# A planned hybrid RWKV-7 / gated DeltaNet block: new planner costs, modulation along the free axis, merged operations, seeded ranks

## The chip, the cores and the metric

The kernel runs on one core of a Trainium2 chip. The metric is the device time in microseconds of one execution; times are given as the median of several runs.

## The reference

One layer of a diffusion backbone over 256 latent tokens and 256 context tokens, with a model width of 2048. All inputs are fp32.

```python
mod = silu_c @ w_ada + b_ada                # 6 x 2048: shift, scale, gate, twice
mod_ctx = silu_cc @ w_ada + b_ada
sh1, sc1, gt1, sh2, sc2, gt2 = split(mod, 6)
h  = modulate(rmsnorm(x, norm1_w), sh1, sc1)
hc = modulate(rmsnorm(ctx, norm1_w), csh1, csc1)
y  = mix_tokens(h, hc, ...)                 # w_in, two mixers, gated merge, w_out
x  = x + gt1 * y
x  = x + gt2 * swiglu(modulate(rmsnorm(x, norm2_w), sh2, sc2), w_gate_up, w_down)
return rmsnorm(x, final_norm_w)
```

`mix_tokens` projects h and hc by `w_in`, runs a bidirectional RWKV-7 scan (16 heads of 64) and a bidirectional chunked gated DeltaNet (8 heads of 128, chunks of 64 here solved in blocks of 128 tokens), where the context's final states start the latent scans, projects both branches, merges them with sigmoid gates and applies `w_out`.

## The kernel before

**Products.** A large product is 128x128 weight tiles against 256 columns of tokens. Each fp32 weight tile is loaded as `wraw`, cast by ScalarE to a rounded high part `whi`, and VectorE subtracts to get the low part `wlo`. Three matmuls (high by high, high by low, low by high) make one fp32-like product. PSUM banks are named `mm` (3), `pa` (2), `pi` (1) and `s` (2).

**Stages by time.** From 0 to about 125 us the norms, the first two parts of the modulation (`ada_first`) and the low-rank columns of `w_in` are computed. From there to about 1340 us one planner, the class `Weave`, writes the instruction order of four engines: RWKV features, inverses and scans for 8 pairs of heads, then DeltaNet features, inverses and scans for 8 heads, with the products of `w_in` and of the merge between them. Then come `w_out` (to about 1440 us) and the FFN, in an order written by hand.

**The planner.** Each piece of work is a generator that yields operations, banks or names of events. `Weave.run` takes, again and again, the operation with the earliest start by its own model, and among equal starts the one with the lower rank. `Lane.cost` models durations, `Loads` (called as `dq`) issues a DMA on SP's queue and returns when the planner expects it to land, `Weave.through` models the fetching of PE's program in pieces. The order is fixed when the kernel is built; on the chip each engine runs its own queue in that order and waits on semaphores. A DMA is issued on SP's queue in the order of the plan too.

Pieces that the change touches:

- `lowrank` and `lowrank_out`: the low-rank products for 8 pairs, their sigmoid on ScalarE into four buffers `lo`, and the write of each to DRAM (`sgd_`), issued on ScalarE's queue.
- `invert`: triangular inverses by 16, 32, 64 blocks; with `full` (DeltaNet) both halves of the last step are made.
- `scan(r)`: four steps, in each of which pair r-1's latent part and pair r's context part run side by side (q is 0 and 1), from state buffers `VX`.
- `tokens`, `head_scan`: the same for DeltaNet, with two directions d.
- `features`: SiLU of a head's q, k, v, then a preload of the table for exp and ln.
- `ada_early`, `ada_rest`, and a last part in the loop over `w_out`: the modulation's columns 4096 to 10240 (gate 1, shift 2, scale 2). A tile has 128 input rows on the partitions and 512 or 1024 output columns; VectorE adds `tile * c[k]` to an accumulator over 16 tiles, and `ada_sum` then sums over the partitions:

```python
yield [e.matmul(ps[32 * j:32 * j + 32, 0:T], ones[:, 0:32], acc[:, T * j:T * j + T], ...) for j in range(nj)]
yield v.tensor_copy(arow[r], ps[r, 0:T])
yield [e.transpose(ps[:, T + P * q:...], arow[r, P * q:P * q + P], ident[r, r]) for q in range(2)]
for q in range(2):
    yield v.tensor_add(mod[:, o], ps[...:32], p_("bada")[:, o])
```

`ada_early` uses two weight buffers that the low-rank part has left (`spare`), and gives them to the ring of weight quarters (`raws`) when it ends.

Of the kernel before, what the change touches and what calls it, by code (L numbers as in the profile page):

```python
# [30 lines left out]
LAT = dict(dma=3.1, v=1.0, s=1.0, hop=dict(e=0.215, v=0.135, s=0.15, g=0.1), slack=0.1, own=0.09, grp=32, crank=-1, cg=4, into=0.14, back=0.2, cross=0.14, stay=0.0, gpace=1.6, fetch=3.7, least=0.2)  # L31
LNEXP = "natural_log_exp_and_others"
SIGM = "sigmoid_and_others"
WAITS = ((0, 1500, 7500, 12000, 13200), (16, 25, 147, 195, 199))
PIECE, EDGE, LEAD = 256, 193, 40
UNIT = 64 * 64 + 64
# [71 lines left out]
class Op:  # L108


    def __init__(self, lane, cost, call, mode=None, base=None, rows=0):
        self.lane, self.cost, self.call, self.mode, self.base, self.rows, self.left = lane, cost, call, mode, base, rows, None


class Lane:


    def __init__(self, engine, fixed, each, own, hop):
        self.engine, self.fixed, self.each, self.own, self.hop, self.base = engine, fixed, each, own, hop + LAT["slack"], None

# [31 lines left out]
    def __getattr__(self, name):  # L152

        def op(out, *a, **k):
            if name == "preload_act_table_set":
                return Op(self, 1.2, lambda: self.engine.preload_act_table_set(out))
            if name == "dma_start":
                return Op(self, 0.6 if self.each > 0.002 else 0.06, lambda: self.engine.dma_start(out, *a))
            mode, base, rows = None, None, rows_of(name, a[0]) if name in ("matmul", "transpose") else 0
# [6 lines left out]
            return Op(self, cost, lambda: getattr(self.engine, name)(out, *a, **k), mode, base, rows)  # L166
        return op
# [27 lines left out]
class Loads:  # L195


    def __init__(self, queue):
        self.queue, self.free = queue, 0.0

    def __call__(self, out, src, slow=1.0):
        self.queue.dma_start(out, src)
# [42 lines left out]
class Weave:  # L245


    def __init__(self):
        self.work, self.free, self.done, self.now, self.mode, self.cur, self.idle = [], {}, {}, 0.0, "full", None, True
        self.counted, self.asked, self.landed = None, -9.0, -9.0  # L250

    def add(self, rank, gen, at=None):
        now, cur = self.now, self.cur
        w = Piece(rank, gen, now if at is None else at)
# [84 lines left out]
    def run(self):  # L339
        while self.work:  # L340
# [40 lines left out]
            for o in ops:  # L381
# [19 lines left out]
def emit(ctx: ExitStack, tc, A, out, dbg=None):  # L401
# [141 lines left out]

    scr = [dpool.tile([2 * 8 * 2 * UNIT], F32, name=f"scr{i}") for i in range(2)]
# [3 lines left out]
    with tc.tile_pool(name="p0", bufs=1) as p0, \  # L548
# [7 lines left out]
        modc = p0.tile([P, 32], F32, name="modc")  # L556
        xt = p0.tile([P, KT, T], F32, name="xt")
# [23 lines left out]
        load_low(0)  # L581

# [125 lines left out]
    def invert(pool, Lt, parts, nu, which, full, fill, half_way=None, early=None):  # L708
# [84 lines left out]
        def out(t, d, h, ps, low):  # L793
# [9 lines left out]
        yield v.tensor_copy(qo, ps[:, 0:32 * h2].rearrange("p (i c) -> p i c", c=32))  # L803
        yield [e.matmul(ps[src, 32 * i:32 * i + 32], qo[dst, i, :], Tx[dst, u, cd], start=True, stop=True)
               for i, h, u, src, dst, cs, cd in quads]
        for h in range(2):
            yield [out(Tx, d, h, ps, True) for d in range(2)]
        weave.release(pib)
        if full:
            ps = yield pib  # L810
            yield [e.matmul(ps[dst, 32 * i:32 * i + 32], Tx[dst, u, cd], qo[dst, i, :], start=True, stop=True)
                   for i, h, u, src, dst, cs, cd in quads]
            for h in range(2):
                yield [out(T0, d, h, ps, False) for d in range(2)]
            weave.release(pib)
# [31 lines left out]
    half = (slice(0, 64), slice(64, 128))  # L847
    pr = [{} for _ in range(NPAIR)]
# [43 lines left out]
    def lowrank():  # L892
# [17 lines left out]
        out = [rs.tile([P, 8, 2, 64], F32, tag=f"VX{i}", name="lo").rearrange("p a b c -> p (a b c)") for i in range(2)]  # L910
        out = [t[:, n:n + 512] for t in out for n in (0, 512)]
# [19 lines left out]
    def prepare(p):  # L931
# [27 lines left out]
        for d in range(2):  # L959
# [19 lines left out]
            if not d:  # L979
# [4 lines left out]
                o["et"] = et = rs.tile([P, 16], F32, tag="et", name="et", bufs=3)  # L984
# [103 lines left out]
    VX = []  # L1088

    def scan(r):  # L1090
# [11 lines left out]
        if not VX:  # L1102
            VX.extend(rs.tile([P, 8, 2, 64], F32, tag=f"VX{i}", name="VX") for i in range(2))
# [12 lines left out]
        for m in range(4):  # L1116
# [6 lines left out]
            for q, o, n, vx, la, cs_ in todo:  # L1123
                for d, j, h in dh:
# [4 lines left out]
            R1 = rs.tile([P, T], F32, tag="y2", name="R1")  # L1129
# [11 lines left out]

            ops = []
# [4 lines left out]
            for q, o, n, vx, la, cs_ in todo:  # L1147
                if n >= 4:
                    for d, j, h in dh:
                        ops.append(add(acc[h, T + 64 * d:T + 64 * d + 64], j, vx[:, 4 * d + cm[d], j, :], la[d][:, cm[d], j, 64:P]))  # L1150
            if ops:
                yield ops
            for q, o, n, vx, la, cs_ in todo:
                for j, h in enumerate(half):
                    yield s.copy(vx[h, both, j, :], c3(ps[h, T + P * q:T + P * q + P]))
# [13 lines left out]
            for q, o, n, vx, la, cs_ in todo:  # L1169
                if n < 7:  # L1170
                    end = o["et"][:, cs_[0]:9 + cs_[1]:8 + cs_[1] - cs_[0]].unsqueeze(2)
                    i = (n + 1) % 4
                    for j, h in enumerate(half):
                        yield v.tensor_mul(VX[0 if n < 3 else 1][h, i:8 - i:7 - 2 * i, j, :], c3(acc[h, P * q:P * q + P]),
                                           end[h].to_broadcast([64, 2, 64]))
# [152 lines left out]
    def products():  # L1328
# [53 lines left out]
        while todo or ahead:  # L1382
# [70 lines left out]
            else:  # L1453
# [9 lines left out]
                  TF0=("VX0", 1024, 1), TF1=("VX1", 1024, 1), St0=("Y", T, 1), St1=("y3", T, 1), arow=("y2", T, 1))  # L1463
    first = {"LAl0": [P, 4, 2, P], "LAl1": [P, 4, 2, P], "LAc0": [P, 4, 2, 64], "LAc1": [P, 4, 2, 64], "Pm": [P, 2, 4, 64],
             "VX0": [P, 8, 2, 64], "VX1": [P, 8, 2, 64], "KBm": [P, 2, 4, 2, 64], "KBc": [P, 2, 4, 2, 64], "ivx": [P, 16, 64], "Y": [P, 4, 64], "R1": [P, 2, 64],
# [49 lines left out]
    def begin():  # L1515
# [48 lines left out]
        yield "scan", NPAIR - 1  # L1564
        for i in range(2):
            tf = gs.tile([P, 8, P], F32, name=f"TF{i}")
            yield g.memset(tf, 0.0)
            TF.append(tf)
# [27 lines left out]
    def features(h):  # L1596
# [16 lines left out]
        yield s.activation(k, k, AF.Silu)  # L1613
        yield s.activation(vq, vq, AF.Silu)
        yield s.preload_act_table_set(LNEXP)
# [4 lines left out]
    def tokens(h):  # L1620
# [18 lines left out]
        for d in range(2):  # L1639
            col = 8 * d + h  # L1640
            yield v.tensor_mul(kta[:, d], p4, eta[:, :, col:col + 1].to_broadcast([P, 4, P]))
# [103 lines left out]
    def head_scan(h):  # L1745
# [13 lines left out]
        for n in range(4):  # L1759
# [15 lines left out]
            for d in range(2):  # L1775
                yield v.tensor_scalar_mul(Vn[:, d, :], ps[:, P * d:P * d + P], btok[:, bs[d], 8 * d + h:8 * d + h + 1])
            weave.release(psb)
            if n < 3:
# [3 lines left out]
                for d in range(2):  # L1782
                    if n:
                        yield v.scalar_tensor_tensor(Sn[:, d, :], St[:, d, :], egl[:, bs[d], 8 * d + h:8 * d + h + 1],
                                                     ps[:, P * d:P * d + P], ALU.mult, ALU.add)
                    else:
                        yield v.tensor_copy(Sn[:, d, :], ps[:, P * d:P * d + P])
                weave.release(psb)
            if n >= 2:
# [3 lines left out]
                for d in range(2):  # L1793
                    y = O[:, bs[d], :]
                    if n == 2:
                        yield s.copy(y, ps[:, P * d:P * d + P])
                    else:
                        yield v.tensor_add(y, ps[:, P * d:P * d + P], y)
# [20 lines left out]
    NEARLY, NLATE = 6, 8  # L1819

    def ada_sum(b, nj, acc, arow):

        m = 2 * nj
        ps = yield pab
        yield [e.matmul(ps[32 * j:32 * j + 32, 0:T], ones[:, 0:32], acc[:, T * j:T * j + T], start=True, stop=True)
               for j in range(nj)]
        weave.ready("block", b)
        r = slice(0, 32 * nj)
        yield v.tensor_copy(arow[r], ps[r, 0:T])
        yield [e.transpose(ps[:, T + P * q:T + P * q + 32 * nj], arow[r, P * q:P * q + P], ident[r, r]) for q in range(2)]  # L1830
        for q in range(2):
            o = slice(32 + b + q, 32 + b + m, 2)
            yield v.tensor_add(mod[:, o], ps[:, T + P * q:T + P * q + 32 * nj:32], p_("bada")[:, o])
        weave.release(pab)
# [334 lines left out]
```

## Time and profile before

| what | value |
|---|---|
| median of 3 runs | 2189.05 us (2185.07 to 2195.54) |
| the profiled execution | 2184.15 us |
| its span | 2182.4 us |
| mean granted TensorE clock | 0.990 |
| instructions | 59116 |
| moved by DMA | 431.14 MB, mean 198 GB/s |

The span runs from the first to the last instruction of the core. PE is TensorE's matmul stream, PEld its weight loads, DVE is VectorE, ACT ScalarE, SP the engine that issues most DMAs; a q behind a name is the engine's sequencer. Nearly all planned operations carry line L166 or L188, those of the helpers that record them, so they are told apart by their tiles. A row of a group gives count, busy time and mean in ns, then the idle time before it and who ended it. A row of a wait gives total, times and longest in us.

### The profile page before, as it was taken

How to read it: one execution, taken by the hardware profiler on the slowest of the kernel's cores; microseconds unless marked ns; L12 is line 12 of the kernel's file. 1: busy time of each engine (PE TensorE's matmuls, PEld its weight loads, DVE VectorE, ACT ScalarE, POOL GpSimd, SP SyncE). 2: the span in 40 equal slices, each digit the busy share in tenths (PEclk: the TensorE clock that was granted, in tenths of full speed). 3: DMA queues.
4: the chain of work that ended last, by engine and by line, in shares of the span. 5: the costliest groups of instructions: out<-in, count | busy, mean ns of one | idle time of the engine just before them, and what ended most of it. 6: DMA issues, size and time to landing. Idle time of an engine off the chain costs nothing.

```text
span 2182.4 us, 59116 instructions
## 1 busy us (share of the span) xinstructions
PE 2104.8 (96%) x24536; PEld 1972.5 (90%) x24536; DVE 1551.1 (71%) x3305; ACT 1118.2 (51%) x2210; POOL 19.2 (1%) x55
## 2 busy tenths in 40 slices
PE   7999999999999999999999998999999999999997
PEld 5897699888898898998989998999999999999997
DVE  4466589889889976899988777865666665555554
ACT  3246655555556556556565755544444444444443
POOL 0000000000000000000000000000000000000000
PEclk9999999999999999999999999999999999999999
DMA  9966756645555554666644746847777776666665
GB/s 376 415 178 195 224 139 184 189 143 154 167 164 149 168 163 141 193 185 178 181 140 116 219 150 197 289 145 223 239 243 236 235 241 212 193 191 194 196 194 164
DMA packets 276813, 431.14 MB, mean 198 GB/s; under 512 B 119872, under 2 KB 137664, under 8 KB 272192
## 3 DMA queue, kind: packets, MB, share of 16 engines
q1 hardware_dynamic: 262720, 402.19, 60.0%
q10 hardware_dynamic: 13824, 25.17, 3.6%
q8 instruction: 192, 3.15, 0.6%
q14 instruction: 77, 0.63, 0.1%
HBM read 401.50 MB, written 25.77 MB: 196 GB/s over the span
## 4 chain that ended last, share of the span: by engine, by line
PE 78%; DVE 8%; DMA 8%; ACT 3%; issue 2%; SPq 0%; ACTq 0%; DVEq 0%
PE mm L188 62%; PE s L188 7%; PE pa L188 5%; PE pi L188 3%; DVE arena L166 2%; DMA wraw<-w 2%; DVE wlo L166 2%; DMA wraw<-ada_rest 1%; DMA wraw<-wgu 1%; ACT whi L166 1%; DMA wraw<-w_low 1%; ACT arena L166 1%; DMA aw<-ada_first 1%; DMA tscr<-arena 1%; DMA sgd__1597<-lo 0%
## 5 line engine op out<-in xcount | busy, mean ns | idle before, releaser
L500 DVE TENSOR_TENSOR wlo<-wraw,whi 128x1024 fp32r<-128x1024 f32 (+1 forms) x264 | 314.9, 1193 | 295.2 <-ACT whi L499 295.1
L499 ACT CAST whi<-wraw 128x1024 fp32r<-128x1024 f32 (+1 forms) x264 | 270.5, 1025 | 389.8 <-PE mm L188 354.8
L188 PE MATMUL mm<-hxh,wlo 128*128 128x256 f32 x1408 | 408.2, 290 | 8.3 <-DVE wlo L166 7.1
L188 PE MATMUL mm<-hxh,whi 128*128 128x256 f32 x1408 | 406.1, 288 | 2.0 <-ACT whi L166 1.0
L188 PE MATMUL mm<-hxl,whi 128*128 128x256 f32 x1408 | 403.9, 287 | 1.4 <-issue 1.4
L188 PE MATMUL mm<-hfh,wlo 128*128 128x256 f32 x1344 | 372.3, 277 | 2.6 <-DVE wlo L500 2.6
L188 PE MATMUL mm<-hfh,whi 128*128 128x256 f32 x1344 | 371.4, 276 | 0.0
L188 PE MATMUL mm<-hfl,whi 128*128 128x256 f32 x1344 | 371.2, 276 | 0.0
L166 ACT CAST whi<-wraw 128x512 fp32r<-128x512 f32 (+1 forms) x399 | 242.9, 615 | 201.1 <-PE mm L188 87.2
L166 DVE TENSOR_TENSOR wlo<-wraw,whi 128x512 fp32r<-128x512 f32 (+1 forms) x399 | 270.3, 680 | 88.5 <-ACT whi L166 85.6
L188 PEld LDWEIGHTS mm<-hxh,wlo 128*128 128x128 f32 x1408 | 266.0, 189 | 19.6 <-DVE wlo L166 11.4
L188 PEld LDWEIGHTS mm<-hxh,whi 128*128 128x128 f32 x1408 | 266.4, 189 | 10.3 <-issue 4.3
L188 PEld LDWEIGHTS mm<-hxl,whi 128*128 128x128 f32 x1408 | 266.2, 189 | 8.1 <-issue 5.7
L188 PEld LDWEIGHTS mm<-hfh,wlo 128*128 128x128 f32 x1344 | 252.4, 188 | 4.2 <-DVE wlo L500 4.0
L188 PEld LDWEIGHTS mm<-hfh,whi 128*128 128x128 f32 x1344 | 252.5, 188 | 0.2 <-ACT whi L499 0.2
L188 PEld LDWEIGHTS mm<-hfl,whi 128*128 128x128 f32 x1344 | 252.5, 188 | 0.0
L188 PE MATMUL mm<-za,whi 128*128 128x256 f32 x1024 | 175.2, 276 | 0.0
L188 PEld LDWEIGHTS mm<-za,whi 128*128 128x128 f32 x1024 | 154.1, 188 | 0.1
L188 PE MATMUL mm<-hch,wlo 128*128 128x256 f32 x528 | 151.1, 286 | 0.0
L188 PE MATMUL mm<-hcl,whi 128*128 128x256 f32 x528 | 150.9, 286 | 0.0
L188 PE MATMUL mm<-hch,whi 128*128 128x256 f32 x528 | 149.9, 284 | 0.0
L188 PE MATMUL mm<-za,wlo 128*128 128x256 f32 x512 | 141.3, 276 | 0.0
(389 smaller groups left out, 4173.4 us busy)
## 6 DMA issues: line engine op xcount, KB each, us to landing
wraw<-w SPq DMA_DIRECT2D x344, 256.0 KB, 3.3
wraw<-wgu SPq DMA_DIRECT2D x168, 512.0 KB, 4.6
aw<-ada_first SPq DMA_DIRECT2D x32, 1024.0 KB, 11.0
wraw<-wdn SPq DMA_DIRECT2D x64, 448.0 KB, 3.7
wraw<-ada_rest SPq DMA_DIRECT2D x96, 256.0 KB, 3.3
aw<-ada_rest SPq DMA_DIRECT2D x48, 512.0 KB, 4.2
wraw<-wout SPq DMA_DIRECT2D x64, 256.0 KB, 5.8
aw<-ada_gt ACTq DMA_DIRECT2D x64, 256.0 KB, 5.1
```

The costliest lines, as they stand in the source:

```text
L166: return Op(self, cost, lambda: getattr(self.engine, name)(out, *a, **k), mode, base, rows)
L188: return f(out, a, *x, **k)
L499: S.copy(hi[:, c, :M], raw[:, c, :M])
L500: V.tensor_sub(lo[:, c, :M], raw[:, c, :M], hi[:, c, :M].bitcast(F32))
```

## The change

- **Planner costs.** `Loads` counts KB, adds a landing time that grows with the transfer and with the KB still on their way; each ScalarE operation carries its table, and a change of table costs 1.28 us. A preload costs nothing else.
- **Seed.** Each piece added before the run and ranked under 800 gets its rank shifted by a number between -2 and 2, drawn with seed 84.
- **Modulation along the free axis.** `ada_rest` is laid out with 128 output columns on the partitions and the 2048 input rows along the free axis. SiLU of c goes to DRAM (`crow`) and is loaded broadcast to all partitions; one VectorE operation multiplies a tile by it and sums the products. `ada_sum` is gone, at all three places.
- **Merged operations.** In `scan`, the two q's state copies and state products become one each; `VX0` and `VX1` become one tile, as do `TF0` and `TF1` and the three `et`. In `tokens` and `head_scan`, two directions go in one operation.
- **Joined lists.** The last step of the full inverse writes both halves in one list, the second into a `pa` bank; the SiLUs and the preload are one list; in `scan` the readout matmuls on old states come ahead of the copy of R1.
- **Low-rank writes** are issued on SP's queue.

```diff
+NUDGE = (84, 2.0)
...
-                return Op(self, 1.2, lambda: self.engine.preload_act_table_set(out))
+                return Op(self, 0.0, lambda: self.engine.preload_act_table_set(out), table=out)
...
     def __call__(self, out, src, slow=1.0):
         self.queue.dma_start(out, src)
-        cost = int(np.prod(out.shape)) * 4 / 360e3 * slow
-        self.free = max(self.free, weave.now) + cost
-        return self.free + LAT["dma"] - weave.now
+        kb = int(np.prod(out.shape)) / 256
+        self.out = [x for x in self.out if x[0] > weave.now]
+        self.free = max(self.free, weave.now) + kb / 400
+        at = max(self.free + 1.8, weave.now + LAT["land"] + 0.0031 * kb + 0.0013 * sum(x[1] for x in self.out))
+        self.out.append((at, kb))
+        return at - weave.now
...
+        if cur is None and rank < 800:
+            rank += NUDGE[1] * (2 * self.draw.random() - 1)
...
+                if o.table is not None and o.table != lane.table:
+                    cost += LAT["table"]
+                    lane.table = o.table
...
-        yield s.dma_start(sgd_[p, :, j], so)
-        yield 2.5
+        yield dq(sgd_[p, :, j], so)
...
-            for q, o, n, vx, la, cs_ in todo:
-                for j, h in enumerate(half):
-                    yield s.copy(vx[h, both, j, :], c3(ps[h, T + P * q:T + P * q + P]))
+            for j, h in enumerate(half):
+                yield s.copy(vxs[h, :, both, j, :], states(ps[h, T + part.start:T + part.stop]))
...
-            for d in range(2):
-                yield v.tensor_scalar_mul(Vn[:, d, :], ps[:, P * d:P * d + P], btok[:, bs[d], 8 * d + h:8 * d + h + 1])
+            b2 = pick(btok.rearrange("p b c -> p (b c)"), 16 * bs[0] + h, 16 * bs[1] + 8 + h)
+            yield v.tensor_mul(Vn, ps[:, 0:T].rearrange("p (d c) -> p d c", d=2), b2.unsqueeze(2).to_broadcast([P, 2, P]))
...
+    def ada_half(w, cB, acc):
+        return v.scalar_tensor_tensor(w, w, 1.0, cB, ALU.mult, ALU.mult, accum_out=acc)
...
+        cB, w = (t.rearrange("p k m -> p (k m)") for t in spare[:2])
+        for q, to in enumerate((mod[:, 32:80], gq)):
+            yield dq(cB, crow[512 * q:512 * q + 512].partition_broadcast(P))
+            for i in range(48):
+                yield dq(w, A["ada_rest"][i, :, 512 * q:512 * q + 512])
+                yield ada_half(w, cB, to[:, i:i + 1])
...
+        yield dq(cB, crow[1024:2048].partition_broadcast(P))
...
+            yield dq(w, A["ada_rest"][i, :, 1024:2048])
+            yield ada_half(w, cB, gr[:, i:i + 1])
...
+                Q.dma_start(w, A["ada_rest"][48 - NLATE + i, :, 1024:2048])
+                V.scalar_tensor_tensor(w, w, 1.0, cB, ALU.mult, ALU.mult, accum_out=gr[:, i:i + 1])
```

More of the change, by code (lines that the diff above doesn't have):

```diff
@@ L1 @@
+import random
 import itertools
@@ L108, with __init__ @@
 class Op:
-    def __init__(self, lane, cost, call, mode=None, base=None, rows=0):
-        self.lane, self.cost, self.call, self.mode, self.base, self.rows, self.left = lane, cost, call, mode, base, rows, None
+    def __init__(self, lane, cost, call, mode=None, base=None, rows=0, table=None):
+        self.lane, self.cost, self.call, self.mode, self.base, self.rows, self.left, self.table = lane, cost, call, mode, base, rows, None, table
 class Lane:
     def __init__(self, engine, fixed, each, own, hop):
-        self.engine, self.fixed, self.each, self.own, self.hop, self.base = engine, fixed, each, own, hop + LAT["slack"], None
+        self.engine, self.fixed, self.each, self.own, self.hop, self.base, self.table = engine, fixed, each, own, hop + LAT["slack"], None, None
     def product(self, out, a):
@@ L155, in op @@
             if name == "preload_act_table_set":
[L156 removed]
+                return Op(self, 0.0, lambda: self.engine.preload_act_table_set(out), table=out)
             if name == "dma_start":
                 return Op(self, 0.6 if self.each > 0.002 else 0.06, lambda: self.engine.dma_start(out, *a))
[L159 removed]
+            mode, base, table, rows = None, None, None, rows_of(name, a[0]) if name in ("matmul", "transpose") else 0
             if name == "transpose" and len(a) == 2:
@@ L165, in op @@
                 cost, base = self.cost(name, out, a, k), (out.offset // out.ap[0][0], out.shape[0])
-            return Op(self, cost, lambda: getattr(self.engine, name)(out, *a, **k), mode, base, rows)
+            if name == "activation":
+                table = TABLES.get(a[1])
+            return Op(self, cost, lambda: getattr(self.engine, name)(out, *a, **k), mode, base, rows, table)
         return op
@@ L542, in emit @@
     S.activation(ck, ck, AF.Silu)
+    crow = dpool.tile([D], F32, name="crow")
     scr = [dpool.tile([2 * 8 * 2 * UNIT], F32, name=f"scr{i}") for i in range(2)]
@@ L556, in emit @@
         modc = p0.tile([P, 32], F32, name="modc")
+        c16 = p0.tile([16, P], F32, name="c16")
+        Q.dma_start(c16, A["cvec"].rearrange("(k p) -> k p", p=P))
+        S.activation(c16, c16, AF.Silu)
         xt = p0.tile([P, KT, T], F32, name="xt")
@@ L803, in invert @@
         yield v.tensor_copy(qo, ps[:, 0:32 * h2].rearrange("p (i c) -> p i c", c=32))
+        pf = (yield pab) if full else None
         yield [e.matmul(ps[src, 32 * i:32 * i + 32], qo[dst, i, :], Tx[dst, u, cd], start=True, stop=True)
-               for i, h, u, src, dst, cs, cd in quads]
+               for i, h, u, src, dst, cs, cd in quads] + [
+            e.matmul(pf[dst, 32 * i:32 * i + 32], Tx[dst, u, cd], qo[dst, i, :], start=True, stop=True)
+            for i, h, u, src, dst, cs, cd in quads if full]
         for h in range(2):
-            yield [out(Tx, d, h, ps, True) for d in range(2)]
+            yield [out(Tx, d, h, ps, True) for d in range(2)] + [out(T0, d, h, pf, False) for d in range(2) if full]
         weave.release(pib)
         if full:
[L810 to L815, printed above, removed]
+            weave.release(pab)
         return N_, Nt_, Tx
@@ L847, in emit, with pick @@
     half = (slice(0, 64), slice(64, 128))
+    def pick(t, i, j):
+        end = j + 1 if j > i else j - 1
+        return t[:, i:None if end < 0 else end:j - i]
+    ets = rs.tile([P, 3, 16], F32, tag="et", name="et")
     pr = [{} for _ in range(NPAIR)]
@@ L909, in lowrank @@
             weave.release(b)
-        out = [rs.tile([P, 8, 2, 64], F32, tag=f"VX{i}", name="lo").rearrange("p a b c -> p (a b c)") for i in range(2)]
-        out = [t[:, n:n + 512] for t in out for n in (0, 512)]
+        out = rs.tile([P, 2, 8, 2, 64], F32, tag="VX", name="lo").rearrange("p i a b c -> p (i a b c)")
+        out = [out[:, n:n + 512] for n in range(0, 2048, 512)]
         for p in range(NPAIR):
@@ L1102, in scan @@
         if not VX:
-            VX.extend(rs.tile([P, 8, 2, 64], F32, tag=f"VX{i}", name="VX") for i in range(2))
+            VXS.append(rs.tile([P, 2, 8, 2, 64], F32, tag="VX", name="VX"))
+            VX.extend(VXS[0][:, i] for i in range(2))
         if more:
@@ L1128, in scan, with add @@
             yield ops
+            acc = yield psb
+            fresh = [True, True]
+            def add(o, j, x, y, stop=False):
+                start, fresh[j] = fresh[j], False
+                return e.matmul(o, x, y, start=start, stop=stop)
+            if last:
+                yield [add(acc[h, T + 64 * d:T + 64 * d + 64], j, vx[:, 4 * d + cm[d], j, :], la[d][:, cm[d], j, 64:P])
+                       for q, o, n, vx, la, cs_ in todo if n >= 4 for d, j, h in dh]
             R1 = rs.tile([P, T], F32, tag="y2", name="R1")
@@ L1168, in scan @@
             yield ops
[L1169 to L1175, printed above, removed]
+            going = [q for q, o, n, *_ in todo if n < 7]
+            if going:
+                i = (m + 1) % 4
+                ends = [(r - 1 + q) % 3 * 16 + m + 4 * q for q in going]
+                ends = [pick(ets.rearrange("p i c -> p (i c)"), x, x + 11 - 2 * m) for x in ends]
+                end = bass.AP(ends[0].tensor, ends[0].offset, [ends[0].ap[0], [ends[-1].offset - ends[0].offset or 1, len(going)], ends[0].ap[1], [0, 64]])
+                to = VXS[0][:, 1 if m == 3 or going[0] == 0 else 0].unsqueeze(1) if len(going) == 1 else VXS[0][:, ::-1]
+                for j, h in enumerate(half):
+                    yield v.tensor_mul(to[h, :, i:8 - i:7 - 2 * i, j, :], states(acc[h, P * going[0]:P * going[-1] + P]), end[h])
             if last:
@@ L1792, in head_scan @@
                        enumerate(((St[:, d, :], Qe[:, d, P * bs[d]:P * bs[d] + P]), (Vn[:, d, :], PT[:, d, bs[d], :])))]
[L1793 to L1798, printed above, removed]
+                y, both = (O if n == 2 else O[:, ::-1]), ps[:, 0:T].rearrange("p (d c) -> p d c", d=2)
+                yield s.copy(y, both) if n == 2 else v.tensor_add(y, both, y)
                 weave.release(psb)
@@ L1815, in head_scan @@
             Q.dma_start(dbg["ob"][:, h, :], ob[:, h, :])
[L1819 to L1834, printed above, removed]
+    NLATE = 8
+    gq = apad[:, 0:48]
+    def ada_half(w, cB, acc):
+        return v.scalar_tensor_tensor(w, w, 1.0, cB, ALU.mult, ALU.mult, accum_out=acc)
     def ada_early():
         yield ("spare",)
-        ws = [t.rearrange("p k m -> p (k m)") for t in spare[:2]]
-        for b in range(NEARLY):
-            for k in range(KT):
-                w, last = ws[k % 2], ws[1 - k % 2]
-                yield dq(w, A["ada_rest"][b // 2, :, k, 512 * (b % 2):512 * (b % 2) + 512])
-                if k:
-                    yield v.scalar_tensor_tensor(w, w, ck[:, k, 0:1], last, ALU.mult, ALU.add)
-                else:
-                    yield s.activation(w, w, AF.Identity, scale=ck[:, 0, 0:1])
-            yield from ada_sum(4 * b, 2, w, last[:, 0:T])
+        cB, w = (t.rearrange("p k m -> p (k m)") for t in spare[:2])
[4 more added lines that the diff above has]
+                yield ada_half(w, cB, to[:, i:i + 1])
         raws.put(*spare[:2])
+        yield v.tensor_add(gq, gq, p_("bada")[:, 32:80])
+        yield v.tensor_add(mod[:, 32:80], mod[:, 32:80], gq)
+        weave.ready("halves")
         yield "turned", NPAIR - 1
@@ L1855, in ada_rest @@
         yield "out", NPAIR - 1
-        acc, kx = [gs.tile([P, 1024], F32, tag="KBc", name="aw") for _ in range(2)]
+        cB, kx = [gs.tile([P, 1024], F32, tag="KBc", name="aw") for _ in range(2)]
         ws = [gs.tile([P, 1024], F32, tag="KBm", name="aw") for _ in range(2)]
@@ L1967, in emit @@
         at = (KT - NB) * NGH // CG
-        acc = mp.tile([P, 1024], F32, name="acc")
-        adds = dict(zip((1, 2, 4, 6, 8, 10, 12, 13), range(KT - NLATE, KT)))
+        cB = mp.tile([P, 1024], F32, name="cB")
+        gr = mp.tile([P, NLATE], F32, name="gr")
+        Q.dma_start(cB, crow[1024:2048].partition_broadcast(P))
+        adds = dict(zip((1, 2, 4, 6, 8, 10, 12, 13), range(NLATE)))
         for j in range(KT):
```

96 lines of the change are left out of this document (32 added, 64 removed).

## The prediction, made before the change was run

> **What bounds the kernel now.** I read the page's busy shares and chain first, then the busy time by stage, then what the tensor engine waited for, then the costliest groups.
>
> ```profile
> span 2182.4 us, 59116 instructions
> PE 2104.8 (96%) x24536; PEld 1972.5 (90%) x24536; DVE 1551.1 (71%) x3305; ACT 1118.2 (51%) x2210; POOL 19.2 (1%) x55
> PE 78%; DVE 8%; DMA 8%; ACT 3%; issue 2%; SPq 0%; ACTq 0%; DVEq 0%
> ```
>
> TensorE is the bound, and 96% busy leaves 77.6 us idle. A busy PE isn't a dense PE, so the idle time is a lower bound for what a better order can recover. Busy time by stage (window, length, PE, PEld, DVE, ACT, POOL, clock, DMA share, GB/s) shows where it lies:
>
> ```profile
> 125.00:260.00 135.00, 126.05 (x909) 100.33 (x910) 80.21 (x175) 83.17 (x155) 2.41 (x7) 0.97 0.65 199
> 260.00:500.00 240.00, 233.21 (x3615) 212.95 (x3614) 211.48 (x497) 130.06 (x332) 6.02 (x18) 1.00 0.58 163
> 500.00:750.00 250.00, 244.43 (x4240) 221.53 (x4239) 226.80 (x533) 136.44 (x358) 8.48 (x23) 1.00 0.57 160
> 750.00:950.00 200.00, 197.72 (x2571) 179.42 (x2568) 156.88 (x385) 123.80 (x283) 1.90 (x2) 0.99 0.58 170
> 950.00:1150.00 200.00, 189.60 (x2350) 176.22 (x2350) 180.98 (x488) 117.47 (x263) 0.00 (x0) 0.97 0.57 163
> 1150.00:1340.00 190.00, 183.87 (x2181) 175.52 (x2179) 146.73 (x398) 108.80 (x239) 0.00 (x0) 0.98 0.56 172
> 1340.00:1440.00 100.00, 95.94 (x819) 92.82 (x817) 80.76 (x138) 60.15 (x108) 0.00 (x0) 1.00 0.80 263
> 1440.00:2182.00 742.00, 726.23 (x6342) 723.29 (x6342) 413.39 (x550) 321.61 (x407) 0.00 (x0) 0.99 0.67 205
> ```
>
> Length less PE busy: 9.0, 6.8, 5.6, 2.3, 10.4, 6.1 in the planned (woven) stretch to 1340, 4.1 in the out projection, 15.8 in the FFN, which the change doesn't touch. So 40 us of PE idle lie where the plan decides. VectorE is 88%, 91% and 90% busy in the windows at 260, 500 and 950: nearly a second bound there. What PE waits for is scattered; the largest waits of 125 to 1440, and ScalarE's largest wait for a transfer (over the span):
>
> ```profile
> PEld s L188 <- ACT lo L166: 12.6, 18, 2.0
> PEld mm L188 <- DVE wlo L166: 11.4, 20, 1.7
> PE mm L188 <- DVE wlo L166: 7.1, 15, 1.5
> ACT whi L166 <- DMA wraw<-w: 73.9, 51, 3.2
> ```
>
> The casts are placed earlier than their quarters land, 51 times, and VectorE's low halves and PE's matmuls queue behind.
>
> **The modulation sums.** Before, a sum over 128 input rows is made by ones-matmuls, a copy, two transposes and two adds, nine times in the woven stretch and once in the out projection. PE's timeline at the first:
>
> ```profile
> 378.17 0.63 PE L188 MATMUL pa<-wraw,CR 128*32 128x256 f32 x4
> 378.73 0.39 PE L188 MATMUL mm<-hxh,wlo 128*128 128x256 f32 x1
> 378.95 0.28 PE L188 MATMUL mm<-hxh,whi 128*128 128x256 f32 x1
> 379.07 0.28 PE L188 MATMUL mm<-hxl,whi 128*128 128x256 f32 x1
> 381.25 0.33 PE L188 MATMUL pa<-C,wraw 64*128 64x64 f32 x2
> 381.51 0.38 PE L188 MATMUL mm<-hxh,whi 128*128 128x256 f32 x1
> ```
>
> The matmuls hold PE from 378.17 to 378.73 (0.56), the next matmul takes 0.22 where 0.12 is usual (0.10 for the return), the transposes 0.26: 0.92 us. Ten of them are 9 us, all on the bound engine: **-9**. A bank of the pair "pa" comes free each time.
>
> What replaces them is the same number of loads and one VectorE operation with an accumulated sum per tile.
>
> ```profile
> L166 DVE SCALAR_TENSOR_TENSOR wraw<-wraw,ck 128x512 f32<-128x512 f32 x90 | 66.8, 743 | 16.2 <-DMA wraw<-ada_rest 15.7
> L166 DVE SCALAR_TENSOR_TENSOR aw<-aw,ck 128x1024 f32<-128x1024 f32 x37 | 47.0, 1270 | 0.0
> L2051 DVE SCALAR_TENSOR_TENSOR aw<-aw,arena 128x512 f32<-128x512 f32 x64 | 41.5, 686 | 0.0
> L2051 DVE DVE_READ_ACCUMULATOR aw<-aw,arena 128x1 f32 x64 | 5.3, 82 | 0.0
> L166 ACT ACTIVATE wraw<-wraw,ck 128x512 f32<-128x512 f32 x6 | 4.3, 724 | 0.1
> L202 SPq DMA_DIRECT2D wraw<-ada_rest x96: 327/328/3016, 248.6 to 933.9; - x96
> ```
>
> L2051 is the same operation already in use for gt2: 686 + 82 ns. Early tiles: 96 x 0.768 = 73.7 against 66.8, so +7 on VectorE. Later ones have no row at 1024 with an accumulator; between 2 x 0.686 and the 1.27 of the scaled form, plus 0.08, I take the nearer form, 1.30 (bounds 1.3 and 1.45): 40 x 1.30 = 52 against 47.0, +5 (at most +11). ScalarE loses nine first tiles, 4.3 us for six. The nine sums' copies (0.42 each, by the rows of that width below) and narrow adds (0.1 each, an estimate) leave VectorE: 9 x 0.62, -5.5. The early loop stays serial, each load behind the last operation, as now: 685 us for 96 loads. The plan's landing grows from 3.8 to 4.1 or more, 96 x 0.3 = 29 us later if that paced it, and six sums leave its chain, each 3.3 us or more by the timeline above; so the two buffers it holds return at about the same time, and I book zero.
>
> [...]
>
> Three broadcast loads of c and its round trip through DRAM are added. In the opening one more SP issue (0.4 us) stands ahead of x; in the out projection 512 KB more pass where the DMA share is 0.80 (2 us at its 263 GB/s). Together between 0 and 3, I take **+1.5**.
>
> **Merged operations.** Rows of the pieces, and rows of the widths that they become:
>
> ```profile
> L166 ACT COPY VX<-s 64x128 f32<-64x128 f32 x128 | 33.2, 260 | 33.8 <-PE s L188 31.5
> L166 ACT COPY VX<-pa 64x256 f32<-64x256 f32 x64 | 23.5, 367 | 8.9 <-PE pa L188 8.1
> L166 DVE TENSOR_TENSOR VX<-s,et 64x128 f32<-64x128 f32 x112 | 32.2, 287 | 9.6 <-PE s L188 7.2
> L166 DVE TENSOR_TENSOR LAc<-pa,C 64x256 f32<-64x256 f32 x32 | 13.5, 421 | 0.7
> L166 DVE TENSOR_SCALAR Vn<-s,btok 128x128 f32<-128x128 f32 x64 | 21.6, 344 | 8.2 <-PE s L188 8.0
> L166 DVE TENSOR_TENSOR arena<-pa,C 128x256 f32<-128x256 f32 x32 | 13.3, 415 | 0.6 <-PE pa L188 0.4
> ```
>
> State copies: 128 become 56 wide and 16 narrow, 56 x 0.367 + 16 x 0.260 = 24.7, -8.5 on ScalarE. State products: 112 become 42 and 28, 42 x 0.421 + 28 x 0.287 = 25.7, -6.5 on VectorE. Vn: 32 x 0.415 = 13.3, -8.3. Outputs, first states and kta also go in pairs, 3.5 on VectorE as an estimate by the same steps (some 0.15 us for each of 24 operations less). VectorE's sum is 7 + 5 - 5.5 - 6.5 - 8.3 - 3.5 = -12. Between no effect (cover by products) and all of it, I take 60%, since half the stretch runs at 90% VectorE: **-7**. The readout matmuls moved ahead of the copy and the shared list of the inverse keep their count; they trade one wait for a bank held longer, bounds -5 to +5, I take 0.
>
> **Low rank writes move from ScalarE's queue to SP's.** ScalarE's timeline in that stage:
>
> ```profile
> 173.44 0.69 ACT L166 ACTIVATE lo<-s,PR 128x512 f32<-128x512 f32 x1 [1.03 <-DMA sgd__1597<-lo]
> 174.16 0.33 ACTq L158 DMA_DIRECT2D sgd__1597<-lo  x1
> 174.59 0.69 ACT L166 ACTIVATE lo<-s,PR 128x512 f32<-128x512 f32 x1 [0.46 <-ACT lo L166]
> 175.29 1.28 ACT L156 ACT_TABLE_LOAD   x1
> 175.31 0.33 ACTq L158 DMA_DIRECT2D sgd__1597<-lo  x1
> 176.59 0.51 ACT L166 ACTIVATE sgd<-raw,om 64x256 f32<-64x256 f32 x1
> ```
>
> Each issue keeps ScalarE from its next operation for 0.46 us: 32 x 0.46 = 15 us in the window 125 to 260. PE's 12.6 us of waiting for "lo" stand against it; a third goes, **-4** (bounds 0 and -12). SP now waits for each activation, with weight loads queued behind it: the slower rival.
>
> **The plan.** The planner now lets a 256 KB quarter land after 4.1 us plus 0.33 for each other one on its way, instead of 3.8; it charges each change of ScalarE's table; the seed shifts ranks by up to 2. None of it is work. Bounds: 0, or a loss like the gain where the new order fits worse, and 40 - 7 - 4 = 29 us, all idle that the other terms leave. I take somewhat over a third of it, since the 51 late casts are what the landing term addresses and most of PE's waits are for other things: **-11**. "Program pieces" stand in the planner already; that part of the title changes nothing.
>
> ```profile
> L166 ACT ACT_TABLE_LOAD x14 | 18.0, 1283 | 1.4 <-DMA arena<-gts__1615 1.2
> ```
>
> These 14 loads, which came with an activation, had no cost in the plan: 18 us of ScalarE that arrived unplanned. In the rows above the load ends at 176.57 and the next activation starts at 176.59, so 1.28 is the whole price, as the plan now has it. [...]
>
> **The sum.** -9 + 1.5 - 7 - 4 - 11 = -29.5 against the profiled execution's 2184.15: 2154.6. The median of the runs is 4.9 above that execution: **2159 us**. About 0.5% (11 us, the runs' own scatter) can't be told from no change.
>
> **Rivals.** (1) The order absorbs the savings: VectorE and ScalarE relief stays under products and the plan's idle only moves. Then PE's 9 us less 1.5 remain: 2189 - 7.5 = 2181. For it: idle is spread over many small waits with no single cause. Against it: VectorE at 90%.
> (2) The plan is better than booked: with true landings the casts run ahead, VectorE's relief counts in full, and PE returns less often from small to full matmuls at 0.1 us each. All 40 us of idle and 9 of sums: 2189 - 49 + 1.5 = 2141, and 15 us less, 2126, if 150 returns fall away. For it: 73.9 us of ScalarE waiting for quarters. Against: only 18 us of PE's waits name "wlo".
> (3) Slower: SP stands at each of the 32 writes until its activation is done, as PE waits for it now up to 2.0 us, and the quarter behind it lands late. 32 x 2.0 = 64 us of SP, which the raw quarters on hand cover in part; if half reaches PE and the plan and ScalarE's relief give nothing, 2189 + 32 - 14.5 = 2206. It decides from 0.45 us of each write on PE (14.5 us, what the sums and VectorE give). Against it: the plan places the write where it expects the activation to end.
>
> **How the numbers follow.** Forecast 0.50 (2142 to 2176), rival 2 0.18, rival 1 0.22 (2178 to 2200), rival 3 0.10. Faster by over 0.5%: 0.50 + 0.18 + a little of rival 1, 0.70; same 0.20; slower 0.10. The range goes from 2128, in rival 2, to 2194, in rival 1, and leaves out rival 3 and the lower half of rival 2, under 2 in 10.
>
> **What would show it.** PE instructions fall by some 80 and no matmul reads ones for the sums; the state copies count 72 and ScalarE's waits for "wraw<-w" fall well under 73.9; PE idle from 125 to 1340 falls from 40 to 25; the FFN stays as it is. The prediction is wrong if SP's own waits grow from 165 to 255 with PE idle there over 9.0, if accumulating tiles take over 0.8 us, or if PE idle before 1340 stays at 40 with VectorE less busy.

## The result, and the profile after

The changed kernel takes 2170.67 us (median of 6 runs, 2165.26 to 2176.36) against 2188.86 for the kernel before beside it: ratio 0.993, interval 0.9906 to 0.9954. That is 18 us of the 29.5 forecast. The head of its page, with the shares of the chain:

```profile
span 2170.1 us, 58874 instructions
PE 2085.1 (96%) x24460; PEld 1963.9 (90%) x24460; DVE 1535.1 (71%) x3335; ACT 1103.2 (51%) x2140; POOL 21.5 (1%) x55
PE 73%; DMA 11%; DVE 9%; ACT 4%; issue 3%; SPq 1%; DVEq 0%; ACTq 0%
```

The span is 12.3 us shorter, PE busy 19.7 less, so PE's idle time grew from 77.6 to 85.0 us. By stage:

```profile
125.00:260.00 135.00, 123.34 (x906) 98.95 (x906) 79.27 (x173) 79.58 (x149) 2.42 (x7) 0.99 0.62 191
260.00:500.00 240.00, 230.02 (x3693) 210.80 (x3691) 209.46 (x511) 126.52 (x311) 7.23 (x20) 0.99 0.58 162
500.00:750.00 250.00, 241.17 (x4169) 219.54 (x4170) 223.51 (x550) 132.71 (x336) 9.58 (x21) 0.99 0.55 156
750.00:950.00 200.00, 196.76 (x2501) 181.43 (x2500) 155.10 (x410) 121.16 (x275) 1.85 (x2) 0.98 0.56 168
950.00:1150.00 200.00, 194.05 (x2471) 184.35 (x2471) 179.38 (x478) 115.28 (x250) 0.00 (x0) 1.00 0.61 184
1150.00:1340.00 190.00, 180.57 (x2106) 171.12 (x2105) 148.00 (x392) 115.51 (x249) 0.00 (x0) 0.97 0.58 179
1340.00:1440.00 100.00, 95.66 (x806) 93.76 (x806) 82.55 (x150) 59.10 (x109) 0.00 (x0) 0.98 0.82 269
```

Length less PE busy is 11.7, 10.0, 8.8, 3.2, 6.0, 9.4 in the planned windows: 49.1 us where 40 stood and 25 were forecast. Only the window at 950 gained. The first FFN matmuls, in the timelines of before and of after, show that the whole gain lies ahead of the FFN:

```profile
1443.26 0.50 PE L188 MATMUL mm<-hfh,w 128*128 128x256 f32 x2 [2.07 <-ACT hfh L2018]
```

```profile
1431.57 0.51 PE L193 MATMUL mm<-hfh,w 128*128 128x256 f32 x2 [2.07 <-ACT hfh L2009]
```

They start 11.7 us earlier; from there to the end it is 739.1 and 738.5 us. The waits of after that answer to those quoted before (the first over the span, the others from 125 to 1440):

```profile
ACT whi L171 <- DMA wraw<-w: 93.7, 57, 6.2
PEld mm L193 <- DVE wlo L171: 18.9, 27, 1.7
PE mm L193 <- DVE wlo L171: 13.2, 23, 1.5
PEld s L193 <- ACT lo L171: 10.8, 19, 2.0
```

In this execution ScalarE waits longer for quarters than before (73.9), and the low halves reach PE later (11.4 and 7.1 before). Its groups show the new operations at their durations:

```profile
L171 DVE SCALAR_TENSOR_TENSOR wraw<-wraw 128x512 f32<-128x512 f32 x96 | 65.9, 687 | 5.0 <-DMA wraw<-ada_rest 4.8
L171 DVE DVE_READ_ACCUMULATOR wraw<-wraw 128x1 f32 x96 | 7.7, 80 | 0.0
L171 DVE SCALAR_TENSOR_TENSOR aw<-aw 128x1024 f32<-128x1024 f32 x40 | 48.3, 1208 | 0.0
L171 ACT COPY VX<-s 64x256 f32<-64x256 f32 (+1 forms) x72 | 24.7, 343 | 26.3 <-PE s L193 25.2
L171 DVE TENSOR_TENSOR VX<-s,et 64x256 f32<-64x256 f32 (+1 forms) x70 | 25.7, 367 | 11.6 <-PE s L193 10.0
L171 DVE TENSOR_TENSOR Vn<-s,btok 128x256 f32<-128x256 f32 x32 | 13.5, 421 | 9.1 <-PE s L193 8.9
L171 ACT ACT_TABLE_LOAD x17 | 21.8, 1283 | 0.9 <-DVE sgd L171 0.7
L207 SPq DMA_DIRECT2D wraw<-ada_rest x96: 327/328/1959, 259.9 to 1152.7; - x96
```

The prices held. The last row didn't: the early loop, whose 96 loads it counts, ends at 1152.7, where it ended at 933.9.

### The profile page after: what moved, and what is told of

It reads as the page before. It is cut to its first block, busy times and chain, and to the rows that moved or that the text cites. A ratio compares the mean times of both kernels' runs of the same rounds, so it can differ in the third digit from the quotient of the medians.

```text
span 2170.1 us, 58874 instructions
## 1 busy us (share of the span) xinstructions
PE 2085.1 (96%) x24460; PEld 1963.9 (90%) x24460; DVE 1535.1 (71%) x3335; ACT 1103.2 (51%) x2140; POOL 21.5 (1%) x55
## 4 chain that ended last, share of the span: by engine, by line
PE 73%; DMA 11%; DVE 9%; ACT 4%; issue 3%; SPq 1%; DVEq 0%; ACTq 0%
PE mm L193 58%; PE s L193 8%; PE pa L193 5%; DMA wraw<-w 3%; PE pi L193 3%; DMA wraw<-wgu 2%; DVE wlo L171 2%; DVE arena L171 2%; ACT whi L171 1%; DVE wlo L514 1%; DMA Tx<-tscr 1%; DMA wraw<-w_low 1%; DMA aw<-ada_first 1%; DMA sgd__1602<-lo 1%; SPq L207 1%
## 5 line engine op out<-in xcount | busy, mean ns | idle before, releaser
L171 ACT CAST whi<-wraw 128x512 fp32r<-128x512 f32 (+1 forms) x399 | 242.9, 614 | 203.1 <-DMA wraw<-w 93.7
```

## The experiments

All ratios are to the kernel before on the same chip. My first theory was that the changed work carries the gain and that orders scatter little; its rivals were that the order chosen by seed 84 carries it, and that the planner's costs do.

**Other seeds for the changed kernel.**

```diff
-NUDGE = (84, 2.0)
+NUDGE = (84, 0.0)   # e1_noseed; e2_seed1: (1, 2.0); e10_seed2: (2, 2.0)
```

> The whole change, but the ranks are not shifted (amplitude 0). Theory W (work): what was gained is TensorE work that is gone, the sums and the returns from small matmuls to full ones; the order only scatters by a few us. It expects 2172 us, between 2166 and 2178, ratio to before 0.990 to 0.995, PE busy about 2085 us as after the change. Theory S (seed): the drawn order carries most of the 18 us. It expects 2182 us or more, ratio 0.997 or above.

> The whole change with another seed (1 in place of 84). Theory W: 2172 us, between 2164 and 2180. Theory S: 84 stands out among orders, so this one is slower by 8 us or more, 2179 to 2195.

> The whole change with seed 2. Theory D: 0.993 to 1.004, as the three orders tried (0.993, 0.997, 1.004). If seed 84 was found by trying many, this one lies above it: 0.996 or more.

Measured: no seed 2181.21 us, 0.9972 (0.9954 to 0.9991); seed 1 2192.62, 1.0037 (1.002 to 1.0054); seed 2 2185.75, 1.0007 (0.9994 to 1.0021). The same work in four orders (seed 84 and these three) spans 1.1%, and with three of four the change would have been measured as under 0.5% either way. The first theory's second half falls.

**The changed kernel once more**, as the reference of that chip; nothing is edited.

> The changed kernel once more, as the reference for the next two on the same chip. The first comparison stands: ratio 0.991 to 0.995. If the 18 us were luck of that chip, 0.997 or above.

2168.16 us, 0.9929 (0.9904 to 0.9955): the result repeats.

**The work with the old planner costs and no seed**, and **the modulation alone**. e3 takes from the diff the modulation along the free axis, the merged operations, the joined lists and the writes on SP's queue; e4 takes the modulation only.

```diff
 # e3_work_only and e4_mod_only: the planner as before
-        at = max(self.free + 1.8, weave.now + LAT["land"] + 0.0031 * kb + ...)
+        return self.free + LAT["dma"] - weave.now
...
-            rank += NUDGE[1] * (2 * self.draw.random() - 1)
...
-                    cost += LAT["table"]
```

> The modulation along the free axis, the merged operations and joined lists and the writes on SP's queue, with the planner's costs and ranks of before (no landing by size, no tables, no seed). Theory W: 2171 us, 2164 to 2178, as fast as the whole change. Theory P (plan): the new costs carry the gain; 2180 us or more. The prediction on record booked 11 us for the plan and seed together, so by it 2181 us.

> Only the modulation along the free axis on the kernel before. Theory W: 9 us of sums leave TensorE and 6 us of its VectorE surplus lie beside them: 2180 us, 2174 to 2184, ratio 0.994 to 0.998, PE busy 9 to 11 us less than the 2104.8 of before. Rival: VectorE, at about 90% in these stretches, takes the accumulated tiles so late that the sums' gain is lost: 2187 to 2193.

e3: 2193.41 us, 1.0033 (1.0014 to 1.0052). e4: 2202.42, 1.0078 (1.005 to 1.0106). Work that is less for PE made the kernel slower than before. e3's page and its clock:

```profile
PE 2092.4 (96%) x24460; PEld 1970.6 (90%) x24460; DVE 1533.3 (70%) x3335; ACT 1100.2 (50%) x2137; POOL 19.5 (1%) x55
```

```profile
core 0: 2187.9 us, clock 0.985
```

e4's:

```profile
PE 2104.3 (96%) x24460; PEld 1976.2 (90%) x24460; DVE 1545.7 (70%) x3433; ACT 1118.1 (51%) x2206; POOL 19.1 (1%) x55
```

```profile
core 0: 2192.6 us, clock 0.985
```

The clock is 0.985 where before and after have 0.990, and PE idles 95.5 and 88.3 us. I therefore split each span into three: PE idle (span less PE busy), clock loss (span times one less the mean clock; the rounding of the clock allows 1.1 us) and the rest, which I call PE's work. The split is that of the profiled execution, which lay off its kernel's median by up to 9.4 us (e11); e4's lay 7.7 below.

**Seeds for the kernel before.** The seed is put into the old planner, with nothing else changed.

```diff
+NUDGE = (84, 2.0)   # e8; e9: (1, 2.0); e11: (2, 2.0)
...
+        if cur is None and rank < 800:
+            rank += NUDGE[1] * (2 * self.draw.random() - 1)
```

> The kernel before with the ranks shifted by seed 84, nothing else. Theory O': the kernel before stands at a good order among its own, and any shift of ranks costs; the new work is faster by some 10 us at like luck. It expects 2189 to 2205, ratio 1.002 to 1.01. Theory S' (seed 84 is good in itself): 2170 to 2180. Theory N (orders of the work before scatter around 1.0): 0.997 to 1.003.

> The kernel before with ranks shifted by seed 1. With seed 84 it came to 1.0107 and the changed kernel with seed 1 to 1.0037. Theory D (draw plus work: each order draws some 0.5% of luck, and the change takes about 10 us at like luck): 1.004 to 1.014, 2192 to 2214. Theory L (draw alone; the change's work is worth nothing and its mean over orders equals that of before): 0.997 to 1.004.

> The kernel before with seed 2, the partner of the run above. Theory D: 1.004 to 1.014 and slower than the changed kernel with seed 2 by 5 us or more. Theory L: as the changed kernel with seed 2 within 5 us or faster.

e8 2206.83 us, 1.0107 (1.0089 to 1.0124); e9 2215.82, 1.0148 (1.0128 to 1.0168); e11 2223.77, 1.0185 (1.0159 to 1.0211). The seed is no gain in itself: 84, the best of the changed kernel's four, costs the kernel before 1.1%. Before's own order is the best of its four. How it and seed 84 were chosen is not on record; if each was picked out of many, neither is a fair draw. The page and the clock of e11, the slowest:

```profile
PE 2123.6 (95%) x24536; PEld 1987.1 (89%) x24536; DVE 1551.5 (70%) x3305; ACT 1126.3 (50%) x2216; POOL 18.8 (1%) x55
```

```profile
core 0: 2231.4 us, clock 0.979
```

The split, in us, each from the span, PE's busy time and the mean clock on its own page:

| kernel | span | PE idle | clock loss | PE's work |
|---|---|---|---|---|
| before | 2182.4 | 77.6 | 21.8 | 2083.0 |
| before, seeds 84, 1, 2 (e8, e9, e11) | 2208.1, 2212.9, 2231.4 | 94.5, 100.3, 107.8 | 37.5, 37.6, 46.9 | 2076.1, 2075.0, 2076.7 |
| modulation alone (e4) | 2192.6 | 88.3 | 32.9 | 2071.4 |
| all work, old costs, no seed (e3) | 2187.9 | 95.5 | 32.8 | 2059.6 |
| after, no seed, seeds 1, 2 (e1, e2, e10) | 2182.1, 2192.4, 2188.2 | 90.3, 92.6, 94.8 | 34.9, 37.3, 35.0 | 2056.9, 2062.5, 2058.4 |
| after, and again (e5) | 2170.1, 2158.8 | 85.0, 79.7 | 21.7, 17.3 | 2063.4, 2061.8 |

PE's work follows the content, with a scatter of 7 to 8 us between orders: 2075 to 2083 before, 2071 with the modulation (one order), 2057 to 2064 with all of it. Idle and clock loss depend on the order: together 99 for before and 97 to 107 for after, 125 to 155 for every other order but e4's, 121. So the time is content plus a draw, and before had a good draw as after has.

Compared at the same seed, before to after, the ratios are 1 to 0.9972 (none), 1.0107 to 0.993 (84), 1.0148 to 1.0037 (1) and 1.0185 to 1.0007 (2): 0.3, 1.8, 1.1 and 1.7% less, 1.2% or 27 us on average. That is near the forecast's 29.5, but it is an average over draws; in it before's mean stands 1.1% above its own order, and after's 0.6% above seed 84, and the 18 us measured is what remains. The same seed doesn't give the same order in both, and the planner's costs differ too, so the pairs are four draws of each and no more.

**The merged operations undone at one order.** The plan stays as it is; where it places a merged operation, its two halves are issued.

```diff
+    def as_(op, *calls):
+        op.call = lambda: [c() for c in calls][-1]
+        return op
...
-                yield s.copy(vxs[h, :, both, j, :], states(...))
+                yield as_(s.copy(vxs[h, :, both, j, :], states(...)),
+                          *[lambda vx=vx, q=q: S.copy(vx[h, both, j, :], c3(...)) for q, ... in todo])
 # likewise the state products, kta, Vn and the DeltaNet outputs
```

> The changed kernel in the very same planned order, but each merged operation of scan, tokens and head_scan (state copies, state products, Vn, kta, outputs) is issued as the two halves that it was made of, and the plan does not know it. Theory M (the merges pay): VectorE has 17 us and ScalarE 10 us more to do at places that TensorE waits on; 7 to 20 us slower than the changed kernel, ratio to before 0.996 to 1.002. Theory O (only the order decides, work of these engines is covered): within 4 us of the changed kernel, 0.991 to 0.995.

2170.81 us, 0.9935 (0.9915 to 0.9954), as e5's 0.9929. Its page:

```profile
PE 2085.9 (96%) x24460; PEld 1963.8 (90%) x24460; DVE 1543.1 (71%) x3425; ACT 1107.8 (51%) x2204; POOL 19.6 (1%) x55
```

VectorE is busy 8.0 us longer with 90 operations more, ScalarE 4.6 longer with 64 more. That is half of what theory M priced: the durations of VectorE's operations add up to 15.2 us more, but the two halves, issued one behind the other, overlap. The median is 2.7 us above e5's, with single runs of e5 between 2159.8 and 2178.8: theory M's 0.996 to 1.002 lies outside the interval, but a loss of a few microseconds can't be told from none.

**The low-rank writes back on ScalarE's queue at one order.**

```diff
+        (queue or self.queue).dma_start(out, src)
...
-        yield dq(sgd_[p, :, j], so)
+        yield dq(sgd_[p, :, j], so, queue=S)
```

> The changed kernel in the same order, but the 32 low-rank writes are issued on ScalarE's queue again, unknown to the plan. The prediction's step: 32 x 0.46 = 15 us of ScalarE, of which 4 us reach TensorE: 4 us slower than the changed kernel, up to 12. Theory O: no difference beyond 2 us. Rival 3 of the prediction (SP stands behind the activations): faster than the changed kernel by 3 us or more.

2170.67 us, 0.9935 (0.9916 to 0.9953). The stage in its trace:

```profile
125.00:260.00 135.00, 121.87 (x870) 95.47 (x870) 79.63 (x174) 79.14 (x148) 2.41 (x7) 0.99 0.61 186
```

PE idles 13.1 us there against 11.7 with the writes on SP. The median is 2.5 us above e5's, within the scatter of single runs, so the 4 us of the step are neither shown nor excluded.

**The modulation sums' matmuls four times**, in the kernel before, its order unchanged and its plan not told.

```diff
-        yield [e.matmul(ps[32 * j:32 * j + 32, 0:T], ones[:, 0:32], ...) for j in range(nj)]
+        ops = [e.matmul(ps[32 * j:32 * j + 32, 0:T], ones[:, 0:32], ...) for j in range(nj)]
+        once = ops[-1].call
+        def again():
+            once()
+            for _ in range(3):
+                for j in range(nj):
+                    x = nc.tensor.matmul(ps[32 * j:32 * j + 32, 0:T], ones[:, 0:32], acc[:, T * j:T * j + T], ...)
+            return x
+        ops[-1].call = again
+        yield ops
```

> The kernel before in its own order, with the ones-matmuls of each of the nine woven sums issued four times in place of once, unknown to the plan (the result is the same). The prediction's step prices one issue at 0.56 us less the return of 0.1, 27 more of them at 12 to 15 us: 2195 to 2199, ratio 1.005 to 1.007. Theory C (TensorE has slack there and the sums are covered): 1.000 to 1.002.

2204.43 us, 1.0089 (1.0074 to 1.0104): 19.4 us (16 to 23) for 27 extra issues, 0.72 each. PE's timeline at the first sum:

```profile
381.27 0.63 PE L190 MATMUL pa<-wraw,CR 128*32 128x256 f32 x4
381.73 1.47 PE L1835 MATMUL pa<-wraw,CR 128*32 128x256 f32 x12
383.12 0.39 PE L190 MATMUL mm<-hxh,wlo 128*128 128x256 f32 x1
```

The three repeats hold PE from 381.73 to 383.12, 1.39 us or 0.46 for one issue; nine sums make 12.5 us. In the profiled execution (span 2206.0, PE busy 2119.9, clock 0.987) the split gives 2091.2 of PE's work, 86.1 of idle and 28.7 of clock loss, which is 8.2, 8.5 and 6.9 more than before. So some two thirds of the loss stand as idle and clock loss; which operations they come from isn't shown. Time put on PE outside the plan was paid in full and more, where 8.0 us put on VectorE or the writes put on ScalarE (e6, e7) cost nothing that these runs resolve.

## Why the forecast was right in sign and too large

The time, 2170.67, lies in the forecast's own interval (2142 to 2176), but that it does is in good part luck: the same work in three other orders took 2181 to 2193 us. Two of the prediction's own signs went against its mechanism: PE idle before 1340 rose from 40 to 49.1 where it was to fall to 25, with VectorE less busy, and ScalarE's wait for quarters didn't fall.

**The sums, -9.** Supported: 0.46 us for an issue of the ones-matmuls beside 0.56 in the prediction's reading, and PE's work falls from a mean of 2077.7 (before in four orders) to 2071.4 with the modulation alone, 6.3 us. Counted from each matmul's start to the next one's, with time at half clock taken as half, the ones-matmuls and the early sums' transposes took 7.2 us in the kernel before, and they are gone in e4. PE's instructions fell by 76 (24536 to 24460; 80 forecast). e4 shows that the gain arrives only in an order that doesn't lose it.

**The broadcast loads, +1.5.** Not resolved: PE idles 4.3 us in the out projection where it was 4.1, and the DMA share there is 0.82 for 0.80.

**VectorE's prices.** Right: 687 and 80 ns for an early tile (686 and 82), 1208 and 80 for a late one (1.29 for 1.30), 24.7 and 25.7 us for the state copies and products (the same), 13.5 for Vn (13.3). The sums' narrow adds, booked at 0.1 us each, took 142 to 161 ns in the kernel before. VectorE's total fell by 16.0, 12 forecast, but that nearness is luck, since two errors cancel: the modulation alone (e4) lowers VectorE's busy time by 5.4 where 6.5 more were booked, and the rest (e3 against e4) by 12.4 where 18.3 were booked. The prediction added up durations, and durations overlap: in e4 they add up to 4.0 more while the busy time, in which an overlap counts once, falls.

**Merged operations, -7.** Not borne out. At a fixed order the halves put 8.0 us on VectorE, not 18.3, and cost no time that the runs resolve (e6), so the bound "no effect" fits as well. "I take 60%, since half the stretch runs at 90% VectorE" took a busy share for a limit. The experiment can't show what the merges did to the planner's choices.

**The moved readouts, 0.** This term, put at nothing with bounds of -5 to +5, carries PE time. In the scan of the kernel before, the readout (`s<-LAl,VX`) stands as a list of its own behind smaller matmuls:

```profile
412.06 0.45 PE L188 MATMUL s<-VX,LAl 128*64 128x64 f32 x8
412.34 0.40 PE L188 MATMUL s<-VX,LAc 128*64 128x64 f32 x8
412.68 0.39 PE L188 MATMUL mm<-hch,wlo 128*128 128x256 f32 x1
414.10 0.39 PE L188 MATMUL s<-VX,C 64*64 64x128 f32 x4
414.42 0.45 PE L188 MATMUL s<-LAl,VX 128*64 128x64 f32 x8
414.80 0.39 PE L188 MATMUL mm<-hch,wlo 128*128 128x256 f32 x1
```

In the changed kernel it follows two lists of the same shape:

```profile
455.51 0.45 PE L193 MATMUL s<-VX,LAl 128*64 128x64 f32 x8
455.79 0.40 PE L193 MATMUL s<-VX,LAc 128*64 128x64 f32 x8
456.02 0.40 PE L193 MATMUL s<-LAl,VX 128*64 128x64 f32 x8
456.36 0.39 PE L193 MATMUL mm<-hxl,whi 128*128 128x256 f32 x1
```

Alone the eight matmuls hold PE for 0.38 us (414.42 to 414.80); as the third list they lengthen the run from 0.62 (412.06 to 412.68) to 0.85, 0.23 more. The matmuls of this shape stand in 102 unbroken runs in all traces without the moved readouts and in 77 in all eight with them, whatever the order; by the count used for the sums they take 49.4 to 50.8 us there and 45.0 to 45.3 here, 4.9 us less. The 25 runs fewer, at the 0.15 us between 0.38 and 0.23, make 3.8 of it. No run moved the readouts alone; that they are the cause is read from their place in these lists.

**Low-rank writes, -4.** Not resolved: e7 is 2.5 us above e5, within the scatter. PE's waits for "lo" fell from 12.6 to 10.8, not by a third, and the 1.8 us can't be followed to the end.

**The early loop, zero.** Wrong as a fact: it ends 219 us later, so the ring gets two buffers late. The prediction let the six sums that leave the chain balance the longer landing. With the old costs the new loop does end earlier, at 906.5 (e4) and 925.2 (e3); with the new costs it ends at 997.0, 1036.3, 1147.8 and 1152.7 in the four orders. So the delay comes with the new costs and the order. Its price wasn't measured; against a large one stands that the fastest of the four orders ends it last, and that the window in which the buffers were missing, 950 to 1150, is the one whose PE idle fell (10.4 to 6.0).

**The plan, -11: the step that failed.** It counted PE's 40 us of idle as stock that a truer plan draws on. PE's idle in these windows rose to 49.1, and none of the other orders of either content idles less than 46: the 40 of the kernel before were already the low end of the draw. ScalarE's wait for quarters was 93.7 instead of falling "well under 73.9"; the same kernel run again (e5) has

```profile
ACT whi L171 <- DMA wraw<-w: 77.0, 48, 5.5
```

so the rise isn't firm, but there is no fall. Nor is this wait a price: it was 54.6 in e4, at 1.0078, and 107.3 in e2, at 1.0037. The median quarter lands 3.4 us from its issue (3.3 before), so the transfers are not slower:

```profile
wraw<-w SPq DMA_DIRECT2D x344, 256.0 KB, 3.4
```

SP itself waits for buffers ahead of its loads, in the kernel before and in the changed one alike:

```profile
SPq L202 <- DVE wlo L166: 229.5, 165, 7.2
```

```profile
SPq L207 <- DVE wlo L171: 237.8, 162, 6.3
```

The prediction read the waits for "wraw<-w" as a landing time put too low; a load that SP issues late would look the same, and which of the two it is, no run separates. What the new costs are worth apart from the draw stays open too: at no seed the time goes from 1.0033 (e3, old costs) to 0.9972 (e1, new costs), 12 us and near the 11 booked, but that is one order each, and four orders of one content differ by more.

**What gave the gain instead.** PE's work fell by 17 us between the means of the two contents (2077.7, and 2060.4 over e3, e1, e2, e10, after and e5). By the count per shape the sums are 7.2 of it and the scan's 128x64 matmuls, with the moved readouts, 4.9. The other 5 are spread over shapes of matmul whose times overlap between the two contents, and I can't put them to a piece of the change; e6 and e7 each keep PE's work low (2066.4 and 2063.6 by the same split), so neither the merged issue nor the queue of the writes is it. Whether the shared list of the inverse has a part wasn't tried. In the profiled pair itself PE's work falls by 19.6 us and 7.4 more of idle stand against it: 12.3 in the spans, 18.2 in the medians.

**The rivals.** The mechanism is nearer to rival 1, "the order absorbs the savings", 2181: e1 gave that time, and e2 and e10 gave more. Rival 2 (2141) has its mechanism in part and none of its idle: matmuls on the whole array that follow smaller ones number 248 to 255 between 125 and 1440 us in the four orders before, 242 in e4 and 226 to 230 with all the work, some 25 fewer and not 150. Rival 3 wasn't seen: from 165 to 255 us the writes make SP wait for "lo" little,

```profile
SPq L207 <- ACT lo L171: 9.4, 15, 1.3
```

where 64 us were feared, and taking them off SP (e7) brought no gain. Table loads of this row went from 14 to 17 at 1283 ns each.

## What to carry to other kernels

When a program is ordered by a planner, one timing of a change is one draw: build the same content in several orders, for the kernel before too, and compare the content and the draw apart (PE's work; PE's idle and clock loss). Relief of an engine beside the bound showed no gain here that could be resolved, 90% busy as it was, while time put on the bound was paid in full: ask for the wait on the bound that names the relieved engine before booking it. Idle time of the bound is stock only if some order is known to have less of it. Lists of small matmuls of one shape are worth putting side by side: the scan's, in 77 runs where there had been 102, took 4.9 us less of TensorE here, in every order and with the same matmuls.

## What the runs showed of the hardware

I had not expected the clock to be part of an order's price. Within the planned stretch the granted clock falls to half, in the traces of before and after for 3.41 or 6.83 us at a time, soon after PE has stood still. In the changed kernel PE stops at 643.10 for 1.38 us in the timeline, and the clock is halved from 646.96 on for 6.83 us:

```profile
641.91 1.19 PE L193 MATMUL pi<-arena 32*32 32x16 f32 x120
644.48 0.25 PE L193 MATMUL pi<-arena 32*32 32x16 f32 x8 [1.38 <-issue]
```

The windows ahead of the stop and in the dip have the clock in the third column from the right, 1.00 and 0.52:

```profile
636.10:642.70 6.60, 6.60 (x146) 6.47 (x148) 5.23 (x9) 0.91 (x2) 0.84 (x2) 1.00 1.00 223
646.70:653.50 6.80, 5.18 (x104) 4.27 (x105) 3.60 (x9) 2.27 (x6) 0.00 (x0) 0.52 0.21 66
```

In the kernel before, two windows around such a dip; 33 matmuls go in the first and 17 in the second, which is as long and has PE busy throughout:

```profile
770.10:773.50 3.40, 3.28 (x33) 3.01 (x32) 0.69 (x1) 1.83 (x7) 0.00 (x0) 1.00 0.79 267
775.70:779.10 3.40, 3.40 (x17) 3.40 (x18) 3.27 (x12) 2.29 (x4) 0.00 (x0) 0.53 0.54 163
```

Counted between 125 and 1480 us in the traces of before, after and the twelve experiments, a dip began within 8 us of the start of 53 of 168 gaps of PE of 0.8 to 1.2 us, 47 of 86 of 1.2 to 1.6, 25 of 41 of 1.6 to 2.0, 38 of 47 of 2.0 to 2.5 and 16 of 19 longer ones. The 152 dips in these 14 stretches of 1355 us would put one within 8 us of some 6% of moments taken at random. Before and after have 8 dips each there, the other six orders of the two 13 to 15; the changed kernel again (e5) has 6, so one order's runs differ in it too. That the gap causes the dip is read from the order in time; no run took a gap away alone. Gaps of 1.2 to 2.5 us were followed by half rate in 110 of 174 cases.
